# Reordering mask, copies, values and fill steps in the attention stage of a hybrid encoder kernel

## The chip, the cores and the metric

The kernel runs on one core of a Trainium2 chip. The metric is the device time of one execution in microseconds; several runs of the same kernel are taken and their median is compared. Five engines work from queues of their own: PE (matrix products; PEld is its weight load), DVE (vector), ACT (scalar functions), POOL (further vector work) and SP, which here issues the DMAs.

## What is computed

One step of an encoder layer with two branches, for a prompt of 1024 frames and for 32 new frames of a running stream that has 512 cached ones. The part that the change touches is attention, 16 heads of width 64, causal, with a bias of cumulative log forget gates:

```python
s = jnp.einsum('bqhd,bkhd->bhqk', q, k)
s = jnp.where(mask, s + bias, finfo.min)
p = jax.nn.softmax(s, axis=-1)
o = jnp.einsum('bhqk,bkhd->bqhd', p, v)
```

Beside it stand a convolution of width 31 over time (`causal_dwconv`), a layer norm over channels of its result, gates, and output projections:

```python
ya = (o_attn * silu(ga)) @ w_pa
yb = (silu(layernorm(conv, ln_g, ln_b)) * silu(gb)) @ w_pb
m = sigmoid(ma) * ya + sigmoid(mb) * yb
return x + m @ w_out
```

All arithmetic is fp32 in effect: a projection is three products of f16 or fp32r halves (`xh`·`wh`, `xh`·`wl`, `xl`·`wh`).

## The kernel before

**Stages.** First come the projections for the convolution, values, keys, queries and the attention gate (up to about 570 us), then the attention stage, then the output projections (`pa`, `pb`, `out`, from about 1052 us). In the attention stage, code written in program order sets the order on PE, DVE, ACT and SP.

**The attention stage** goes over `seq`, 132 items: for each head eight blocks of 128 queries (`Block(head, i)`, i from 0 to 7, with (i+1)·128 keys), and four items for the running stream (`Sample(g)`, four heads at a time), each put behind block 0 of heads 3, 7, 11 and 15. An item goes through these steps:

- `scores` (L1108 on): PE computes the scores into a PSUM tile `psS` (two buffers); then, in the same method, DVE adds the causal mask to the diagonal (L1124) and takes the negated row maximum `nm` (L1126).
- `soft`: ACT takes the exponential from `psS` into `P` and sums the rows (L1133).
- `norm`: DVE takes the reciprocal of the sum (L1138), POOL multiplies `P` by it (L1139).
- `turn`: PE transposes `P` in pieces of 128 keys into `psT` tiles `ptr` (L1153; two banks, up to four pieces in each). ACT copies the first bank out (L1156), DVE the second, which exists from block 4 on (the same line).
- `values`: at block 7 of a head, PE multiplies the turned blocks of the whole head with `V` (`po`, L1172) into two `psT` banks; ACT copies one half of the rows out (L1176), DVE adds the other (L1177) and, for odd heads, multiplies by the gate (L1179), which a DMA loads when block 5 comes by.
- `finish`: for the running stream alone.

The loop is a pipeline: iteration `n` does the scores, mask and maximum of item n+3, the turn of item n, the exponential of n+3, the reciprocal of n+2, two fill steps, the values of n-2, and two fill steps more.

**Fill.** `fill(n)` takes n steps from a generator that computes the remaining gate projections (`gb`, `ma`, `mb`): one step is three products of 128x352 on PE (L183). A step also calls `beat()`, which issues work that was set for that time: loads, squares and splits of weights (`junk`, `wh` on ACT, `wl` on DVE), and the taps of the convolution on DVE (L371), at a rate of `R_A` taps per step. `NFILL` gates give 528 steps in all. Twelve are taken ahead of the loop; the loop takes four per iteration, and none at blocks 0 to 2 of head 8.

**Layer norm.** Once the last tap's sums are there, each iteration also advances `layernorm()` by one step (22 steps): products with a matrix of ones into `psT` (`psn`, L1202) for mean and variance, and then Newton's steps on DVE.

```python
some = 2 if isinstance(b, Sample) or b.i > 2 or b.head.h != 8 else 0
fill(some)
if n >= 2 and pending(seq[n - 2]):
    seq[n - 2].values()
fill(some)
```

Of the kernel before, what the change touches and what calls it, by code (L numbers as in the profile page):

```python
# [8 lines left out]
F32 = mybir.dt.float32  # L9
# [5 lines left out]
ALU = mybir.AluOpType  # L15
AX = mybir.AxisListType

D = 1024
T = 1024
# [6 lines left out]
CH = 352  # L26
# [4 lines left out]
LNO = ((0,), (1, 2), (3,), (4, 5), (6,), (7,), ())  # L31
LNEXP = "natural_log_exp_and_others"
NFILL = 22
R_U, R_V, R_QK, R_G, R_A = 0.21, 0.18, 0.165, 0.23, 0.2
NWARM = 34
HT = TT // 2
HC = HT // 2
# [16 lines left out]
def build(tc, xT, xt, wv, wf, ckT, cv, clT, stT, vec, cst, yT, kT, vO, lfO, cpT, csT):  # L54
    nc = tc.nc
# [3 lines left out]
    def pool(name, bufs=1, stack=es, **kw):  # L59
        return stack.enter_context(tc.tile_pool(name=name, bufs=bufs, reuse_waits="tile", **kw))  # L60
# [19 lines left out]
    rstd = lnp.tile([128, TT], F32, name="rstd")  # L80
# [105 lines left out]
    def csl(c):  # L186
        return slice(c * CH, (c + 1) * CH)
# [88 lines left out]
    def t352(name, bufs):  # L276
        return sg.tile([128, CH], F32, name=name, tag=name, bufs=bufs)
# [5 lines left out]
    class Banks:  # L283

        n = 0
# [221 lines left out]
    def newton(out, v, y):  # L507

        nc.vector.tensor_mul(out, y, y)
        nc.vector.scalar_tensor_tensor(out, out, -0.5, v, op0=ALU.mult, op1=ALU.mult)  # L510
        nc.vector.scalar_tensor_tensor(out, out, 1.5, y, op0=ALU.add, op1=ALU.mult)
# [225 lines left out]
    for c in range(4):  # L737
# [16 lines left out]
        for t in range(8):  # L754
            ps = pj.tile([128, 512], F32, name="pjv", tag="pj")
            n = 0
            for kt in range(KT):
                sl = slice(t * 128, t * 128 + 128)
# [243 lines left out]
    psT = pool("psT", 2, stack=p2, space=PS)  # L1002
# [4 lines left out]
    class Two:  # L1007
        n = 0
# [14 lines left out]
    def fill(n):  # L1023
        for _ in range(n):
            next(flow, None)

    class Sample:
# [15 lines left out]
        def scores(self):  # L1043
            g, kc, pf = self.g, self.kc, self.pf
            ps = psS.tile([128, 2, 512], F32, name="psS", tag="S")
            for j in range(4):
                rows = slice(64 * (j % 2), 64 * (j % 2) + 64)
                q = qs_t[rows, 2 * g + j // 2, :]
                nc.tensor.matmul(ps[32 * j:32 * j + 32, 0, :], q, kc[rows, j // 2, :], start=True, stop=True)
                nc.tensor.matmul(ps[32 * j:32 * j + 32, 1, :TS], q, ks_t[rows, 2 * g + j // 2, :],  # L1050
                                 start=True, stop=True)
            nc.vector.scalar_tensor_tensor(pf[:, :PAST], ps[:, 0, :], cq[:, g:g + 1], pf[:, :PAST],
                                           op0=ALU.add, op1=ALU.subtract)
            nc.vector.scalar_tensor_tensor(pf[:, PAST:], ps[:, 1, :TS], cq[:, g:g + 1], pf[:, PAST:],
                                           op0=ALU.add, op1=ALU.subtract)
            nc.vector.tensor_add(pf[:, PAST:], pf[:, PAST:], smask)
            self.nm = nm = ap.tile([128, 3], F32, name="nm", tag="nm", bufs=6)
            nc.vector.tensor_reduce(nm[:, 0:1], pf, axis=AX.X, op=ALU.max, negate=True)
# [45 lines left out]
    class Block:  # L1104
# [5 lines left out]
        def scores(self):  # L1110
            i = self.i
            QA, QB, KA, KB = self.head.q
            nk = (i + 1) * 128
            qsl = slice(i * 128, i * 128 + 128)
            ps = psS.tile([128, 2, 512], F32, name="psS", tag="S")
            nb = 1 if nk <= 512 else 2
            w = nk // nb
            wm = max(w, 256)
            for b in range(nb):
                ksl = slice(b * w, b * w + wm)  # L1120
                nc.tensor.matmul(ps[:, b, :wm], QB[:, qsl], KB[:, ksl], start=True, stop=False)  # L1121
                nc.tensor.matmul(ps[:, b, :wm], QA[:, qsl], KA[:, ksl], start=False, stop=True)  # L1122
            diag = ps[:, nb - 1, w - 128:w]
            nc.vector.tensor_add(diag, diag, cmask)  # L1124
            nm = ap.tile([128, 3], F32, name="nm", tag="nm", bufs=6)
            nc.vector.tensor_reduce(nm[:, 0:1], ps[:, :nb, :w], axis=AX.XY, op=ALU.max, negate=True)  # L1126
            self.at = ps, nm, nk, nb, w
# [55 lines left out]
    seq = []  # L1183
# [5 lines left out]
    def start(b):  # L1189
        if getattr(b, "i", 1) == 0:  # L1190
            h = b.head
            if h.h % 2 == 0:
                h.ot = heads[h.h + 1].ot = ap.tile([128, T], F32, name="ot", tag="ot", bufs=2)
        b.scores()

    def pending(b):
        return isinstance(b, Sample) or b.i % 2

    def over_channels(acc, put):
        for c in range(3):  # L1200
            pm = psT.tile([128, 512], F32, name="psn", tag="T")
            nc.tensor.matmul(pm[:, :CH], ones_f, acc[:, csl(c)], start=True, stop=True)  # L1202
            put(csl(c), pm[:, :CH])
            yield

    def layernorm():

        shift = sides["shift"]
        for _ in range(4):
            yield  # L1210
        yield from over_channels(mean, lambda sl, ps: nc.scalar.mul(mean[:, sl], ps, 1.0 / D))

        def put(sl, ps):
            t = t352("t", 3)
            nc.scalar.activation(t, mean[:, sl], AF.Square)
            nc.vector.scalar_tensor_tensor(rstd[:, sl], ps, 1.0 / D, t, op0=ALU.mult, op1=ALU.subtract)
            nc.vector.tensor_add(mean[:, sl], mean[:, sl], shift[:, sl])
            nc.vector.tensor_scalar(rstd[:, sl], rstd[:, sl], EPS, None, op0=ALU.add)

        yield from over_channels(rstd, put)  # L1220
        for c in range(6):
            sl = slice(c * CH // 2, c * CH // 2 + CH // 2)
            v, y = rstd[:, sl], t352("t", 3)[:, :CH // 2]
            nc.scalar.activation(y, v, AF.Ln)
            nc.scalar.activation(y, y, AF.Exp, scale=-0.5)
            yield
            w = t352("t", 3)[:, :CH // 2]
            nc.vector.tensor_copy(w, v)
            newton(v, w, y)
            yield  # L1230

    ones_f = cp.tile([128, 128], F32, name="ones_f", tag="ob")
    nc.vector.memset(ones_f, 1.0)
    ln = layernorm()
    sides["shift"] = ap.tile([128, TT], F32, name="shift", bufs=1)
    nc.sync.dma_start(sides["shift"], s_m)
    heads[1].load()
    for n in range(3):
        start(seq[n])
        seq[n].soft()  # L1240
        if n:
            seq[n - 1].norm()
        fill((8, 4, 0)[n])
    for n, b in enumerate(seq):
        if n + 3 < len(seq):
            start(seq[n + 3])
        if n + 9 < len(seq) and getattr(seq[n + 9], "i", 1) == 0:
            seq[n + 9].head.load()
        if n + 6 < len(seq) and isinstance(seq[n + 6], Sample):
            seq[n + 6].load()  # L1250
        if getattr(b, "i", 0) == 3 and b.head.h + 1 < H:
            heads[b.head.h + 1].load_v()
        b.turn()
        if n + 3 < len(seq):
            seq[n + 3].soft()
        if n + 2 < len(seq):
            seq[n + 2].norm()
        some = 2 if isinstance(b, Sample) or b.i > 2 or b.head.h != 8 else 0
        fill(some)
        if n >= 2 and pending(seq[n - 2]):  # L1260
            seq[n - 2].values()
        fill(some)
        if n >= 3 and isinstance(seq[n - 3], Sample):
            seq[n - 3].finish()
        if "ready" in sides:
            next(ln, None)
# [17 lines left out]
    class Banks3:  # L1284
        n = 0
# [383 lines left out]
```

## Time and profile before

| what | value |
|---|---|
| median of 3 runs | 1349.14 us (1349.07 to 1354.99) |
| profiled execution, its own time | 1345.89 us |
| its span | 1344.1 us |
| PE busy | 1312.6 us (98%) |
| DVE busy | 990.4 us (74%) |
| ACT busy | 719.0 us (53%) |
| POOL busy | 505.8 us (38%) |
| mean granted PE clock | 0.996 |

The span is the stretch that the profiler recorded; the time of the same execution is 1.8 us longer. A group row gives line, engine, operation, output<-inputs, shapes and count, then busy time and mean duration in ns, then the engine's idle time ahead of these instructions and what ended it. A row of the timeline gives start, duration, and in brackets the idle time before it with its releaser. Matmul ends are modelled and overlap the next matmul, so that a short stall of PE may not show as idle time.

### The profile page before, as it was taken

Reading aid. Unit: us, or ns where it says so; the run is one execution under the profiler, and the core shown is the slowest. Engines: PE = TensorE matmul, PEld = TensorE weight load, DVE = VectorE, ACT = ScalarE, POOL = GpSimd, SP = SyncE. Lnnn points to the kernel's source line nnn. Section 1 sums busy time; section 2 is a strip of 40 time slices with the busy share of each in tenths; the row PEclk is TensorE's granted clock in tenths of the full one; section 3 lists DMA queues with packets and bytes.
Section 4 is the critical chain, followed back from the end, with each engine's and each line's share of the span. In section 5 each row is a group of like instructions: output and inputs, shape, how many; then the busy total and the mean of one; then the engine's idle time right before and its main releaser. Section 6 shows DMA issues by size and latency. Waiting matters only on the chain.

```text
span 1344.1 us, 24837 instructions
## 1 busy us (share of the span) xinstructions
PE 1312.6 (98%) x9383; PEld 1003.1 (75%) x9383; DVE 990.4 (74%) x1532; ACT 719.0 (53%) x1362; POOL 505.8 (38%) x548
## 2 busy tenths in 40 slices
PE   8999999999999999999889998999999999999999
PEld 5687876666666666667567766777776699999998
DVE  6797879888999997987778866655554489166664
ACT  6644555757676743455555555655555566233320
POOL 2001124547484820243433442222222158255562
PEclk8999999999999999999999999999999999999999
DMA  6343233425352463535644643565452698544462
GB/s 251 98 140 104 93 112 118 139 82 187 95 180 87 162 166 109 160 90 155 165 109 123 186 132 99 147 179 132 131 152 54 240 313 262 176 128 146 142 190 69
DMA packets 113496, 194.97 MB, mean 145 GB/s; under 512 B 34080, under 2 KB 80032, under 8 KB 113376
## 3 DMA queue, kind: packets, MB, share of 16 engines
q1 hardware_dynamic: 113232, 193.31, 46.9%
q8 instruction: 74, 1.21, 0.4%
q14 instruction: 46, 0.38, 0.1%
q10 hardware_dynamic: 144, 0.07, 0.0%
HBM read 127.68 MB, written 65.64 MB: 144 GB/s over the span
## 4 chain that ended last, share of the span: by engine, by line
PE 82%; DVE 9%; ACT 3%; issue 2%; DMA 2%; SPq 1%; POOL 0%; DVEq 0%; ACTq 0%; POOLq 0%
PE pj L183 56%; PE pjv L761 6%; PE pj L1501 6%; PE po L1172 4%; PE ptr L1153 3%; DVE nm L1126 2%; DVE wl L141 2%; DVE y L371 2%; PE psS L1122 2%; PE psS L1121 2%; DMA ga<-s_ga 2%; ACT wh L138 1%; DVE psS L1124 1%; DMA s_q<-qh 1%; PE warm L477 1%
## 5 line engine op out<-in xcount | busy, mean ns | idle before, releaser
L183 PE MATMUL pj<-xh,wh 128*128 128x352 f16 (+2 forms) x1536 | 481.6, 314 | 2.3 <-ACT wh L138 1.4
L183 PE MATMUL pj<-xh,wl 128*128 128x352 f16 (+2 forms) x1536 | 481.2, 313 | 0.7 <-DVE wl L141 0.6
L183 PE MATMUL pj<-xl,wh 128*128 128x352 f16 (+2 forms) x1536 | 480.9, 313 | 0.5 <-DVE xl L579 0.4
L183 PEld LDWEIGHTS <-wh 128*128 128x128 f16 x3072 | 301.5, 98 | 162.1 <-issue 7.1
L371 DVE SCALAR_TENSOR_TENSOR y<-u,vec_t,y 128x1086 f32<-128x1086 f32 x240 | 346.8, 1446 | 12.0 <-ACT y L368 8.9
L1139 POOL TENSOR_SCALAR P<-P,nm 128x128 f32<-128x128 f32 (+7 forms) x128 | 129.9, 1015 | 279.9 <-DVE nm L1138 229.8
L183 PEld LDWEIGHTS <-wl 128*128 128x128 f16 x1536 | 150.5, 98 | 72.0 <-DVE wl L141 1.6
L141 DVE SCALAR_TENSOR_TENSOR wl<-raw,sc,wh 128x384 f16<-128x384 f32 (+1 forms) x192 | 128.2, 693 | 48.3 <-ACT wh L138 48.3
L1133 ACT ACTIVATE P<-psS,nm 128x128 f32<-128x128 f32 (+7 forms) x128 | 95.1, 743 | 113.3 <-DVE nm L1138 70.9
L1126 DVE TENSOR_REDUCE nm<-psS 128x1 f32<-128x128 f32 (+7 forms) x128 | 97.0, 758 | 12.5
L1153 PE MATMUL ptr<-ident,P 128*128 128x128 f32 x576 | 88.6, 276 | 17.3 <-DVE pt L1156 9.2
L175 POOL TENSOR_TENSOR wl<-raw,wh 128x384 fp32r<-128x384 f32 (+1 forms) x51 | 63.3, 1270 | 74.3 <-ACT wh L172 58.6
L1153 PEld LDWEIGHTS ptr<-ident,P 128*128 128x128 f32 x576 | 69.2, 141 | 28.2 <-DVE pt L1156 12.1
L1156 ACT COPY pt<-ptr 128x512 f32<-128x512 f32 (+3 forms) x128 | 64.3, 502 | 44.4 <-PE ptr L1153 43.2
L1121 PE MATMUL psS<-KB,QB 128*128 128x256 f32 (+2 forms) x192 | 81.8, 427 | 0.6 <-ACT P L1133 0.6
L880 POOL TENSOR_TENSOR sql<-sqf,sqh 128x352 fp32r<-128x352 f32 x48 | 57.0, 1187 | 65.8 <-ACT sqh L877 65.8
L138 ACT ACTIVATE wh<-raw,sc 128x1024 f16<-128x1024 f32 (+1 forms) x68 | 73.9, 1091 | 8.2 <-DVE sc L158 7.9
L1172 PE MATMUL po<-pt,V 128*64 128x256 f32 x640 | 72.8, 382 | 2.5 <-ACT pts L1078 1.7
L1124 DVE TENSOR_TENSOR psS<-psS,cmask 128x128 f32<-128x128 f32 x128 | 37.6, 294 | 46.0 <-PE psS L1122 45.6
L906 POOL TENSOR_TENSOR ql<-qn,qh 128x352 fp32r<-128x352 f32 (+1 forms) x48 | 67.8, 1429 | 6.6 <-ACT qh L905 6.5
L761 PE MATMUL pjv<-vwh,xh 128*128 128x260 f16 x256 | 70.1, 274 | 0.0
L761 PE MATMUL pjv<-vwl,xh 128*128 128x260 f16 x256 | 70.0, 273 | 0.0
(271 smaller groups left out, 2532.9 us busy)
## 6 DMA issues: line engine op xcount, KB each, us to landing
raw<-wf SPq DMA_DIRECT2D x92, 512.0 KB
QB<-s_q SPq DMA_DIRECT2D x32, 256.0 KB
KB<-s_k SPq DMA_DIRECT2D x32, 256.0 KB
kT<-qn SPq DMA_DIRECT2D x8, 528.0 KB
s_ga<-t SPq DMA_DIRECT2D x24, 176.0 KB
s_gb<-t SPq DMA_DIRECT2D x24, 176.0 KB
s_ma<-t SPq DMA_DIRECT2D x24, 176.0 KB
s_mb<-t SPq DMA_DIRECT2D x24, 176.0 KB
```

Of the source, the lines that this page charges most:

```text
L138: nc.scalar.mul(wh[:, ks, :], raw[:, ks, :], self.s[:, i:i + 1])
L141: nc.vector.scalar_tensor_tensor(wl[:, ks, :], raw[:, ks, :], self.s[:, i:i + 1], wh[:, ks, :], op0=ALU.mult, op1=ALU.subtract)
L183: nc.tensor.matmul(ps, a[:, kt, :], b(kt, sl), start=(first and n == 0), stop=(last and n == N - 1))
L371: t = nc.vector.scalar_tensor_tensor(y, u[:, i:i + CW], w, y, op0=ALU.mult, op1=ALU.add)
L761: nc.tensor.matmul(ps[:, :VC], a, b, start=(n == 0), stop=(n == 23))
L1121: nc.tensor.matmul(ps[:, b, :wm], QB[:, qsl], KB[:, ksl], start=True, stop=False)
L1126: nc.vector.tensor_reduce(nm[:, 0:1], ps[:, :nb, :w], axis=AX.XY, op=ALU.max, negate=True)
L1133: nc.scalar.activation(P[:, :nk].rearrange("p (b w) -> p b w", b=nb), ps[:, :nb, :w], AF.Exp, bias=nm[:, 0:1], accum_out=nm[:, 1:2])
L1139: nc.gpsimd.tensor_scalar(P[:, :nk], P[:, :nk], nm[:, 2:3], 1.0, op0=ALU.mult, op1=ALU.mult)
L1153: nc.tensor.transpose(pt[:, 128 * j:128 * j + 128], P[:, 128 * (4 * u + j):128 * (4 * u + j) + 128], ident)
L1172: nc.tensor.matmul(po[rows], V[:, j, :], parts[c][:, j, :], start=(c % 2 == 0 and j < 2), stop=(c % 2 == 1 and j >= 2 * c))
L1501: nc.tensor.matmul(pss[c][:, :HC], a[:, k, :], x, start=(not more and kt == 0 and n == 0), stop=(kt == 3 and n == 2), skip_group_check=more)
```

## The change

Five things are edited in the attention stage.

- `scores` is cut in two in both classes: PE's products stay in `scores`, the mask and the maximum on DVE go to a new method `top`. In the loop `scores` of item n+3 still stands ahead of the turn of item n, `top` behind it.
- The reciprocal of item n+2 (`norm`) moves to the front of the iteration.
- `values` of item n-2 moves ahead of the exponential of item n+3 and of all fill steps.
- The four fill steps stand together; blocks 0 to 2 of head 8 get them too, and block 6 of heads 2 to 13 takes three.
- `R_A` goes from 0.2 to 0.165, and the layer norm's variance step yields between the square on ACT and the product on PE.

The loads that stood ahead of the turn now stand behind it.

```diff
-R_U, R_V, R_QK, R_G, R_A = 0.21, 0.18, 0.165, 0.23, 0.2
+R_U, R_V, R_QK, R_G, R_A = 0.21, 0.18, 0.165, 0.23, 0.165
...
                 nc.tensor.matmul(ps[:, b, :wm], QA[:, qsl], KA[:, ksl], start=False, stop=True)
+            self.at = ps, nk, nb, w
+
+        def top(self):
+            ps, nk, nb, w = self.at
             diag = ps[:, nb - 1, w - 128:w]
             nc.vector.tensor_add(diag, diag, cmask)
             nm = ap.tile([128, 3], F32, name="nm", tag="nm", bufs=6)
...
-        def put(sl, ps):
+        for c in range(3):
+            sl = csl(c)
             t = t352("t", 3)
             nc.scalar.activation(t, mean[:, sl], AF.Square)
-            nc.vector.scalar_tensor_tensor(rstd[:, sl], ps, 1.0 / D, t, op0=ALU.mult, op1=ALU.subtract)
+            yield
+            pm = psT.tile([128, 512], F32, name="psn", tag="T")
+            nc.tensor.matmul(pm[:, :CH], ones_f, rstd[:, sl], start=True, stop=True)
+            nc.vector.scalar_tensor_tensor(rstd[:, sl], pm[:, :CH], 1.0 / D, t, op0=ALU.mult, op1=ALU.subtract)
...
     for n, b in enumerate(seq):
+        if n + 2 < len(seq):
+            seq[n + 2].norm()
         if n + 3 < len(seq):
             start(seq[n + 3])
+        b.turn()
+        if n + 3 < len(seq):
+            seq[n + 3].top()
...
-        b.turn()
+        if n >= 2 and pending(seq[n - 2]):
+            seq[n - 2].values()
         if n + 3 < len(seq):
             seq[n + 3].soft()
-        if n + 2 < len(seq):
-            seq[n + 2].norm()
-        some = 2 if isinstance(b, Sample) or b.i > 2 or b.head.h != 8 else 0
-        fill(some)
-        if n >= 2 and pending(seq[n - 2]):
-            seq[n - 2].values()
-        fill(some)
+        fill(3 if getattr(b, "i", 0) == 6 and 2 <= b.head.h < 14 else 4)
```

How this moves instructions is shown at three places. On DVE, at blocks 4 and 5 of head 0 (`ptr_7044` and `ptr_7084` are the second banks of their turns), the order before was:

```order
L1124 TENSOR_TENSOR psS<-psS,cmask 128x128
L1126 TENSOR_REDUCE nm<-psS 128x1
L1156 COPY pt<-ptr_7044 128x128
L1138 RECIPROCAL nm<-nm 128x1
L141 SCALAR_TENSOR_TENSOR wl<-raw,sc,wh 128x384
L371 SCALAR_TENSOR_TENSOR y<-u,vec_t,y 128x1086
L141 SCALAR_TENSOR_TENSOR wl<-raw,sc,wh 128x384
L1124 TENSOR_TENSOR psS<-psS,cmask 128x128
L1126 TENSOR_REDUCE nm<-psS 128x1
L1156 COPY pt<-ptr_7084 128x2x128
```

and it now is, at the same two blocks (`ptr_7042`, `ptr_7082`; lines are shifted by 8):

```order
L1146 RECIPROCAL nm<-nm 128x1
L1164 COPY pt<-ptr_7042 128x128
L1132 TENSOR_TENSOR psS<-psS,cmask 128x128
L1134 TENSOR_REDUCE nm<-psS 128x1
L141 SCALAR_TENSOR_TENSOR wl<-raw,sc,wh 128x384
L371 SCALAR_TENSOR_TENSOR y<-u,vec_t,y 128x1086
L141 SCALAR_TENSOR_TENSOR wl<-raw,sc,wh 128x384
L1146 RECIPROCAL nm<-nm 128x1
L1164 COPY pt<-ptr_7082 128x2x128
```

The copy has moved ahead of mask and maximum, the reciprocal ahead of the copy; taps and weight splits stand between the maximum of one block and the reciprocal of the next, as before.

On PE, at block 1 of head 8, where the values of head 7 are computed, the order before was (no fill step follows):

```order
L1153 MATMUL ptr_9761<-ident,P 128x128 x2
L1172 MATMUL po<-pt,V 64x256 x20
L1202 MATMUL psn<-rstd,ones_f 128x352
L1121 MATMUL psS<-KB,QB 128x384
L1122 MATMUL psS<-KA,QA 128x384
```

and it now is:

```order
L1161 MATMUL ptr_9735<-ident,P 128x128 x2
L1180 MATMUL po<-pt,V 64x256 x20
L183 LDWEIGHTS wh
L183 MATMUL pj<-xh,wh 128x352
L183 LDWEIGHTS wl
L183 MATMUL pj<-xh,wl 128x352
```

Fill steps now follow the values, and the layer norm's products come between one and two heads later. At other heads two fill steps stood between the transposes and `po`; now none does.

On ACT, at the running stream's first item (its turn's copies are the two `pts` rows), the order before was:

```order
L1078 COPY pts<-ptr_7940 128x512
L1081 COPY pts<-ptr_7946 32x128
L1133 ACTIVATE P,nm<-psS,nm 128x512
L1176 COPY ot<-po 64x512 x2
L1156 COPY pt<-ptr_8001 128x2x128
```

and it now is:

```order
L1082 COPY pts<-ptr_7929 128x512
L1085 COPY pts<-ptr_7935 32x128
L1184 COPY ot<-po 64x512 x2
L1141 ACTIVATE P,nm<-psS,nm 128x512
L948 ACTIVATE t<-pj,sc 128x352
```

The exponential stands behind the two copies of `po`, so it waits for PE to finish the values.

More of the change, by code (lines that the diff above doesn't have):

```diff
@@ L1051, in scores @@
                                  start=True, stop=True)
+            self.ps = ps
+        def top(self):
+            g, ps, pf = self.g, self.ps, self.pf
             nc.vector.scalar_tensor_tensor(pf[:, :PAST], ps[:, 0, :], cq[:, g:g + 1], pf[:, :PAST],
@@ L1122, in scores, with top @@
                 nc.tensor.matmul(ps[:, b, :wm], QA[:, qsl], KA[:, ksl], start=False, stop=True)
+            self.at = ps, nk, nb, w
+        def top(self):
+            ps, nk, nb, w = self.at
             diag = ps[:, nb - 1, w - 128:w]
@@ L1211, in layernorm @@
         yield from over_channels(mean, lambda sl, ps: nc.scalar.mul(mean[:, sl], ps, 1.0 / D))
-        def put(sl, ps):
+        for c in range(3):
+            sl = csl(c)
             t = t352("t", 3)
             nc.scalar.activation(t, mean[:, sl], AF.Square)
-            nc.vector.scalar_tensor_tensor(rstd[:, sl], ps, 1.0 / D, t, op0=ALU.mult, op1=ALU.subtract)
+            yield
+            pm = psT.tile([128, 512], F32, name="psn", tag="T")
+            nc.tensor.matmul(pm[:, :CH], ones_f, rstd[:, sl], start=True, stop=True)
+            nc.vector.scalar_tensor_tensor(rstd[:, sl], pm[:, :CH], 1.0 / D, t, op0=ALU.mult, op1=ALU.subtract)
             nc.vector.tensor_add(mean[:, sl], mean[:, sl], shift[:, sl])
             nc.vector.tensor_scalar(rstd[:, sl], rstd[:, sl], EPS, None, op0=ALU.add)
-        yield from over_channels(rstd, put)
         for c in range(6):
@@ L1239, in build @@
         start(seq[n])
+        seq[n].top()
         seq[n].soft()
```

## The prediction

> **What bounds the kernel now.** I read the page's head first, then the table of windows by head, then the waits of the stage that the change touches.
>
> ```profile
> span 1344.1 us, 24837 instructions
> PE 82%; DVE 9%; ACT 3%; issue 2%; DMA 2%; SPq 1%; POOL 0%; DVEq 0%; ACTq 0%; POOLq 0%
> ```
>
> The second line is the chain of waits by engine: PE sets 82% of the end, DVE 9%. All edits lie in the attention stage, 576 to 1052 us. From the windows (PE, PEld, DVE, ACT, POOL busy with counts, then the granted clock):
>
> ```profile
> 576.00:664.00 88.00, 80.63 (x571) 58.00 (x571) 69.48 (x132) 50.12 (x108) 36.68 (x41) 1.00 0.50 137
> 664.00:785.00 121.00, 115.03 (x861) 83.08 (x861) 96.19 (x182) 64.99 (x141) 46.32 (x54) 1.00 0.49 135
> 785.00:900.00 115.00, 109.35 (x801) 79.28 (x802) 69.66 (x174) 68.65 (x154) 31.66 (x55) 0.99 0.53 143
> 900.00:1052.00 152.00, 149.86 (x1157) 108.62 (x1157) 79.70 (x194) 83.90 (x181) 36.48 (x66) 1.00 0.43 117
> 726.50:754.00 27.50, 27.41 (x198) 20.09 (x198) 23.35 (x42) 16.83 (x38) 13.27 (x14) 1.00 0.41 105
> 816.20:849.00 32.80, 28.78 (x186) 20.56 (x188) 21.68 (x53) 17.92 (x42) 7.25 (x12) 0.95 0.49 120
> ```
>
> PE idles 476 - 454.9 = 21.1 us here: 7.4 + 6.0 + 5.7 in the first three windows, 2.1 in the last. DVE is 79% busy up to 785 us (165.7 of 209), when its conv taps run, and 52% after 900. A head without disturbance (fifth row) takes 27.5 us; the head whose values end the sixth row's stretch takes 32.8, although three blocks in it have no fill. What PE waited for in the stage:
>
> ```profile
> PE ptr L1153 <- DVE pt L1156: 9.2, 11, 1.7
> PE ptr L1153 <- ACT pt L1156: 6.4, 5, 2.2
> PE po L1172 <- ACT pts L1078: 1.7, 2, 0.9
> PE ptr L1153 <- DVE ot L1177: 1.2, 1, 1.2
> PE po L1172 <- ACT mean L1211: 0.7, 1, 0.7
> PE psS L1121 <- ACT P L1133: 0.6, 2, 0.4
> ```
>
> So most of the loss is transposes (`ptr`) waiting for a `psT` bank that DVE or ACT has not yet copied out, hardly ever scores waiting for an exponential (0.6 us).
>
> **Term 1, the copy ahead of mask and maximum.** One such wait, engine by engine:
>
> ```profile
> 647.05 1.04 DVE L141 SCALAR_TENSOR_TENSOR wl<-raw,sc,wh 128x256 f16<-128x256 f32 x1
> 648.02 0.29 DVE L1124 TENSOR_TENSOR psS<-psS,cmask 128x128 f32<-128x128 f32 x1
> 648.41 1.22 DVE L1126 TENSOR_REDUCE nm<-psS 128x1 f32<-128x1024 f32 x1
> 649.55 0.28 DVE L1156 COPY pt<-ptr 128x128 f32<-128x128 f32 x1
> 649.89 0.33 PE L1153 MATMUL ptr<-ident,P 128*128 128x128 f32 x1 [1.16 <-DVE pt L1156]
> ```
>
> The copy of block 4 stands 1.53 us (648.02 to 649.55) behind a mask and maximum for another block. Moved ahead, it would have ended before PE asked. The other starts:
>
> ```profile
> 590.97 0.29 DVE L1124 TENSOR_TENSOR psS<-psS,cmask 128x128 f32<-128x128 f32 x1
> 591.57 0.41 DVE L1156 COPY pt<-ptr 128x256 f32<-128x256 f32 x1
> 592.04 0.55 PE L1153 MATMUL ptr<-ident,P 128*128 128x128 f32 x3 [1.74 <-DVE pt L1156]
> 691.24 0.29 DVE L1124 TENSOR_TENSOR psS<-psS,cmask 128x128 f32<-128x128 f32 x1
> 691.97 0.55 DVE L1156 COPY pt<-ptr 128x384 f32<-128x384 f32 x1
> 692.57 0.66 PE L1153 MATMUL ptr<-ident,P 128*128 128x128 f32 x4 [1.27 <-DVE pt L1156]
> ```
>
> Block 5's copy gains only 0.60 us and block 6's 0.73, since the maximum in front belongs to a small block. By these three amounts, four waits for block 4's copy vanish, three for block 5's lose 0.5 us each, four for block 6's 0.68 each: about 7 of the 9.2 us (told apart by the number of transposes that waited: 1 or 2, 3, 4). From below the term is 0 (PE comes earlier to a DVE that is just as busy). I take 5.5, near the upper end, because the waits after a block are single and short, and a copy in front is in front every time.
>
> **Term 2, the fill steps.** Four steps are twelve matmuls:
>
> ```profile
> 742.25 1.79 PE pj L183 x12
> 816.20 4.11 PE L1172 MATMUL po<-pt,V 128*64 128x256 f32 x36 [0.65 <-ACT mean L1211]
> 823.48 0.52 PE L1153 MATMUL ptr<-ident,P 128*128 128x128 f32 x3 [1.25 <-DVE ot L1177]
> 824.57 0.86 PE L1202 MATMUL psn<-rstd,ones_f 128*128 128x352 f32 x2 [0.57 <-ACT pt L1156]
> 834.27 0.33 PE L1153 MATMUL ptr<-ident,P 128*128 128x128 f32 x1 [2.20 <-ACT pt L1156]
> 826.00:828.00 2.00, 2.00 (x9) 1.45 (x9) 0.64 (x2) 1.33 (x4) 0.80 (x1) 0.50 0.89 199
> ```
>
> A step is 1.79 / 4 = 0.45 us. Head 8's three empty blocks get 12 steps, 5.4 us of PE work, where PE idled 0.65 + 1.25 + 0.57 + 2.20 = 4.7 us and where the granted clock fell (last row: 0.50 for 2 us, so 1 us more). Twelve other heads give up one step each at block 6. If head 8's stalls took up the work whole, the gain would be 5.4 us plus that 1 us; if the givers are held by DVE anyway, as the heads before 785 us partly are, only half of the twelve pay. I take 4.5, bounds 2 and 6.5. [...]
>
> **Term 3, values ahead of the whole fill.** PE now goes from the turn's transposes straight to `po`, with two fill steps (0.9 us) less for the copies, and four steps instead of two behind it. The wait of 1.25 at 823.48 (already counted) shows what four steps behind would cover. Against it stands the one place without fill ahead, the 0.65 us at 816.20. Worst are the four running-stream blocks, whose turn uses both `psT` banks:
>
> ```profile
> 663.27 0.58 ACT L1078 COPY pts<-ptr 128x512 f32<-128x512 f32 x1
> 663.90 4.54 PE L1172 MATMUL po<-pt,V 128*64 128x256 f32 x40 [0.94 <-ACT pts L1078]
> ```
>
> ACT is late there by itself, so the wait grows by the whole 0.9 us at the two blocks that wait today and by 0 to 0.9 at the other two: -1.8 to -3.6, taken as -2.7. The twelve plain heads need their second bank only after the first six of twenty products (0.3 of 4.54 us, 1.4 us later), so I put 0.1 us on each, bounds 0 and 0.65: -1.2 (0 to -7.8).
>
> **Term 4, reciprocal first, pace, layer norm.** R_A from 0.2 to 0.165 takes 0.035 x 4 = 0.14 taps from each block while taps last:
>
> ```profile
> L371 DVE SCALAR_TENSOR_TENSOR y<-u,vec_t,y x41: 1328/1333/2207, 579.5 to 772.7; 128x1086 f32<-128x1086 f32 x41
> 649.75 1.12 ACT L1133 ACTIVATE P<-psS,nm 128x1024 f32<-128x1024 f32 x1 [1.79 <-DVE nm L1126]
> 641.19 0.52 PE L1121 MATMUL psS<-KB,QB 128*128 128x512 f32 x1
> 642.24 0.60 PE L1153 MATMUL ptr<-ident,P 128*128 128x128 f32 x4
> L138 ACT ACTIVATE wh<-raw,sc 128x1024 f16<-128x1024 f32 x22 | 25.1, 1140 | 0.0
> L1133 ACT ACTIVATION_READ_ACCUMULATOR P<-psS,nm 128x1 f32 x128 | 25.0, 195 | 0.0
> L1138 DVE RECIPROCAL nm<-nm 128x1 f32<-128x1 f32 x128 | 19.6, 153 | 0.2 <-ACT P L1133 0.2
> ```
>
> At 1.33 us a tap that is 0.19 us per block, some 11 us of DVE time over the 57 blocks until 772 us, given back after it, where DVE has room; the last taps and the 22 layer-norm steps still end well inside the 132 blocks. What PE gets of it is between 0 and the 4 us of DVE waits that the first two windows would otherwise keep or see return; I take +2. The reciprocal, 0.15 us, never waited before (0.2 us over 128). At the head of DVE's block it can: it waits for the exponential of two blocks on, and copy, mask and maximum wait behind it. At block 4 the loop is copy 0.28, mask and maximum 1.53, exponential 1.12, accumulator 0.2, reciprocal 0.15: 3.3 us. PE's own block is the fill's 1.79, four score products (641.19 to 642.24, 1.05) and five transposes, about 0.6: 3.4. They nearly tie, so I charge 0.03 us for each of 64 blocks with a DVE copy, -2; from 0 to -20 (0.31 each). The layer norm's extra yield moves a wait of DVE for a square; PE does not see it. No DMA is added; the loads of a head come one turn later on SP, with several blocks to spare, and the fill steps after 1052 us are the same.
>
> **Sum.** 5.5 + 4.5 - 2.7 - 1.2 + 2 - 2 = 6.1 us from single waits. The displayed idle of 21.1 leaves out what a stall hides under the modelled tails of matmuls: the 32.8 us after 816.2 lack six fill steps (the other six lie before it), so they are 32.8 - (27.5 - 2.7) = 8.0 over a plain head, of which 1.3 are three `psn` products (0.86 for two passes, some half of it tail) and 1 the clock: 5.7, against 4.0 displayed in it (1.25 + 0.57 + 2.20). That ratio is 1.4; I let the 10 us of terms 1 and 2 grow by 1.3, to 13, and the sum to 9. On the profiled execution 1344.1 becomes 1335 (its time 1345.9 becomes 1337). The median of the runs, 1349.1, lies 3.2 above that one, so I forecast 1349 - 9 = **1340 us**.
>
> **Rivals.** (a) *The banks were the whole trouble*: DVE's copy waits, ACT's (6.4 us) and the hole all go, about 21 of idle less 4 of new waits: 1349 - 18 = 1331. For it: the clean head at 27.5 us with DVE 85% busy. Against: the ACT waits have other causes. (b) *The copy does not come sooner where it counts*: in rows like 591.57 taps and `wl` stand ahead of mask and copy alike, term 1 gives 2 and the new `po` waits 5; with the hole 4.5 and the pace 2 that leaves 3.5: 1345.5. For it: the longest wait, 1.74, keeps 1.1 even by my own count. (c) *The loop decides, and it is slower*: reciprocal, copy, maximum and exponential form a ring through DVE and ACT, and at the end of a head the exponential also stands behind two copies of `po` on ACT, 4.5 us later. If each of 64 large blocks loses 0.14 us beyond the 0.03 charged (the 9 us), the gain is gone; at 0.31 the kernel stands at 1349 - 9 + 20 = 1360. For it: the tie above, and 22 `wh` splits of 1.14 us on the same ACT queue. Against: scores have two buffers and waited 0.6 us in all, and blocks 0 to 3 need no DVE copy, so a lag is made good there. [...]
>
> **How the numbers follow.** My forecast (1335 to 1345) has 0.50, (a) 0.15, (b) 0.22, (c) 0.13. What a measurement of this kernel tells from no change is about 0.5%, 6.7 us: faster means below 1342.4, slower above 1355.9. Faster takes 0.47 of the 0.50 and all of (a): 0.62; same is the rest and (b): 0.25; slower is (c): 0.13. For 8 in 10 the range goes from inside (a), 1329, to beyond (b), 1351.
>
> **What would show it.** Right: PE's waits for DVE `pt` fall from 9.2 below 4 us, the granted clock stays 1.00 around head 8, its stretch of 32.8 us shrinks below 30, and `po` <- ACT `pts` rises by 2 to 3 us. Wrong: reciprocals or copies on DVE with idle time put down to ACT's exponential, scores waiting for ACT `P` by many times 0.6 us, or new `po` waits at plain heads beyond 0.3 us each; and if the stage's idle falls while its length does not, the sum from displayed waits was the mistake.

## The result and the profile after

The changed kernel takes 1361.32 us (median of 5 runs, 1360.73 to 1363.06), the one before 1350.59 (5 runs, 1349.07 to 1354.99): a ratio of 1.0074, 95% interval 1.0052 to 1.0097. It is slower by some 10 us; 1340 was forecast, and the time lies where rival (c) stood. The profiled execution, at 1363.1 us, is the longest of the five, while that of the kernel before, at 1345.9, is shorter than all of its five, so the two traces lie 17 us apart where the medians lie 11 apart. Sizes are therefore taken from ratios below, and the traces are used to see where things moved.

From the page of the changed kernel, its span and the chain of waits by engine:

```profile
span 1361.3 us, 24814 instructions
PE 78%; DVE 8%; ACT 4%; DMA 4%; issue 3%; SPq 2%; POOL 0%; DVEq 0%; ACTq 0%; POOLq 0%
```

PE's share of the chain fell from 82 to 78%. The loss is in the attention stage, which here runs from 576 to 1069 us; the columns are the stretch, its length, busy time of PE, PEld, DVE, ACT and POOL with counts, the granted clock, DMA share and GB/s:

```profile
576.00:1069.00 493.00, 463.51 (x3392) 331.29 (x3392) 315.56 (x684) 266.58 (x582) 122.64 (x215) 0.99 0.47 127
```

It is 17 us longer than the 476 before. PE's idle time rose from 21.1 to 29.5 us, and PE's busy time by another 8.7 for the same matmuls (3392 records and 3386). What PE waited for there:

```profile
PE po L1180 <- ACT pts L1082: 8.0, 4, 2.7
PE ptr L1161 <- ACT pt L1164: 7.2, 9, 1.6
PE psS L1125 <- ACT P L1141: 3.5, 5, 1.1
PE po L1180 <- ACT pt L1164: 2.5, 4, 1.3
PE ptr L1161 <- ACT mean L1219: 2.2, 2, 1.2
PE ptr L1161 <- DVE pt L1164: 1.7, 2, 1.2
PE ptr L1084 <- ACT pt L1164: 1.6, 1, 1.6
```

The wait for DVE's copy fell from 9.2 to 1.7 us, just as term 1 had it. Head 8's stretch, from the values of head 7 at 821.0 to its own at 851.2 us, takes 30.2 us where it took 32.8, and its clock stays at 1.00. In their place stand waits for ACT: for the running stream's copy (`pts`) 8.0 instead of 1.7, at plain heads 2.5 for the second bank (`po` <- ACT `pt`) instead of none, for the turned copies 7.2 instead of 6.4, and scores waiting for an exponential 3.5 instead of 0.6. Some 5 of the 8.7 us of busy time are the clock, by an estimate from the slices below (6.5 us lost, less 1.7 before). These are slices of the changed kernel at three of the four running-stream items:

```profile
660.00:670.00 10.00, 5.83 (x27) 3.25 (x29) 6.35 (x9) 4.31 (x10) 5.18 (x8) 0.69 0.86 196
910.00:920.00 10.00, 7.93 (x50) 5.11 (x50) 4.50 (x14) 4.67 (x12) 1.81 (x5) 0.83 0.70 168
1030.00:1040.00 10.00, 7.49 (x46) 4.74 (x48) 3.67 (x10) 4.07 (x11) 1.46 (x4) 0.83 0.12 41
```

The granted clock is 0.69, 0.83 and 0.83 there, over ten us each: 3.1 + 1.7 + 1.7 = 6.5 us of clock lost. Before, one slice of the stage alone had such a clock, at head 8, for 1.7 us:

```profile
820.00:830.00 10.00, 8.18 (x40) 5.42 (x37) 6.34 (x14) 3.40 (x7) 1.01 (x2) 0.83 0.34 100
```

The first of the three places, in the timeline (start, duration, engine, instruction, idle time before it and its releaser):

```profile
659.25 0.60 PE L1081 MATMUL ptr<-ident,pf 128*128 128x128 f32 x4
...
659.84 1.35 DVE L371 SCALAR_TENSOR_TENSOR y<-u,vec_t,y 128x1086 f32<-128x1086 f32 x1 [1.88 <-ACT y L368]
...
661.45 0.29 PE L1084 MATMUL ptr<-ident,pf 128*32 128x128 f32 x1 [1.61 <-ACT pt L1164]
...
662.22 0.58 ACT L1141 ACTIVATE P<-psS,nm 128x384 f32<-128x384 f32 x1 [0.81 <-DVE nm L1134]
662.69 0.19 ACT L1141 ACTIVATION_READ_ACCUMULATOR P<-psS,nm 128x1 f32 x1
662.79 1.04 ACT L117 ACTIVATE junk<-raw 128x1024 bf16<-128x1024 f32 x1
...
663.83 0.57 ACT L1082 COPY pts<-ptr 128x512 f32<-128x512 f32 x1
...
664.45 7.52 PE L1180 MATMUL po<-pt,V 128*64 128x256 f32 x40 [2.71 <-ACT pts L1082]
```

ACT copies the turn's first bank 4 us after PE filled it: it stands behind an exponential that itself waited for DVE's maximum, and behind a square of weights (`junk`). DVE was late with that maximum because a tap of the convolution stood in front, which had itself waited 1.88 us for ACT. PE has only `po` next, so it idles 1.61 and 2.71 us with one transpose between, and then the values run at the reduced clock (0.69 from 660 to 670 us): 7.52 us where the same 40 records took 4.54 before.

### The profile page after: what moved, and what is told of

It reads as the page before. It is cut to its first block, busy times and chain, and to the rows that moved or that the text cites. A ratio compares the mean times of both kernels' runs of the same rounds, so it can differ in the third digit from the quotient of the medians.

```text
span 1361.3 us, 24814 instructions
## 1 busy us (share of the span) xinstructions
PE 1320.1 (97%) x9383; PEld 1004.8 (74%) x9383; DVE 987.4 (73%) x1532; ACT 716.3 (53%) x1362; POOL 475.0 (35%) x548
## 4 chain that ended last, share of the span: by engine, by line
PE 78%; DVE 8%; ACT 4%; DMA 4%; issue 3%; SPq 2%; POOL 0%; DVEq 0%; ACTq 0%; POOLq 0%
PE pj L183 54%; PE pjv L761 6%; PE pj L1512 6%; PE po L1180 4%; PE ptr L1161 3%; DMA ga<-s_ga 2%; DVE nm L1134 2%; PE psS L1125 2%; PE psS L1126 2%; ACT wh L138 1%; DVE wl L141 1%; DVE y L371 1%; DMA s_y<-y 1%; ACT P L1141 1%; DVE psS L1132 1%
## 5 line engine op out<-in xcount | busy, mean ns | idle before, releaser
L1147 POOL TENSOR_SCALAR P<-P,nm 128x128 f32<-128x128 f32 (+7 forms) x128 | 95.8, 749 | 277.7 <-DVE nm L1146 220.2
L1180 PE MATMUL po<-pt,V 128*64 128x256 f32 x640 | 80.3, 407 | 10.6 <-ACT pts L1082 8.0
L1180 PEld LDWEIGHTS po<-pt,V 128*64 128x64 f32 x640 | 46.8, 145 | 40.0 <-ACT pts L1082 9.1
L761 PE MATMUL pjv<-vwh,xl 128*128 128x260 f16 x256 | 69.9, 273 | 0.0
```

What stands on the lines that cost most here:

```text
L761: nc.tensor.matmul(ps[:, :VC], a, b, start=(n == 0), stop=(n == 23))
L1147: nc.gpsimd.tensor_scalar(P[:, :nk], P[:, :nk], nm[:, 2:3], 1.0, op0=ALU.mult, op1=ALU.mult)
L1180: nc.tensor.matmul(po[rows], V[:, j, :], parts[c][:, j, :], start=(c % 2 == 0 and j < 2), stop=(c % 2 == 1 and j >= 2 * c))
```

## The experiments

All ratios are to the kernel before, run on the same chip in turn with it. The expectations name theories: S (the four running-stream items lose cover and clock), V (values first cost at every head, through the exponential behind two copies of `po`), L (the loop of reciprocal, copy, maximum and exponential, rival (c)).

**e1: values back between the fill steps, in the changed kernel.**

```diff
-        if n >= 2 and pending(seq[n - 2]):
-            seq[n - 2].values()
         if n + 3 < len(seq):
             seq[n + 3].soft()
-        fill(3 if getattr(b, "i", 0) == 6 and 2 <= b.head.h < 14 else 4)
+        some = 3 if getattr(b, "i", 0) == 6 and 2 <= b.head.h < 14 else 4
+        fill(2)
+        if n >= 2 and pending(seq[n - 2]):
+            seq[n - 2].values()
+        fill(some - 2)
```

> The changed kernel with one part undone: values stand between two fill steps and the rest again, and the exponential ahead of them on ACT; all else as changed. Theory S (the four running-stream items: po waits 8.0 us for ACT's pts copy where it waited 1.7, and the granted clock falls to 0.50 for some 5 us behind three of them): both go back, 1361 to about 1349, po's wait for pts under 2.5 us and no slice of the clock below 0.9 in the attention stage. Theory L (the loop of reciprocal, copy, maximum, exponential on all large blocks): the time stays within 3 us of 1361, since the loop is left as it is.

Measured: 1351.25 us, ratio 1.0004 (0.9993 to 1.0016). PE's wait for `pts` fell to 4.0 us, and in the profiled execution, the shortest of ten, only one slice of ten us in the stage (830 to 840) has a clock below 0.98. The place of the values is worth some 9 us; `pts` stayed above the 2.5 that was expected. What is left of the change gains nothing on the kernel before.

**e2: two fill steps ahead of the values at the running stream's items alone, in the changed kernel.**

```diff
+        some = 3 if getattr(b, "i", 0) == 6 and 2 <= b.head.h < 14 else 4
+        if isinstance(b, Sample):
+            fill(2)
+            some -= 2
         if n >= 2 and pending(seq[n - 2]):
             seq[n - 2].values()
         if n + 3 < len(seq):
             seq[n + 3].soft()
-        fill(3 if getattr(b, "i", 0) == 6 and 2 <= b.head.h < 14 else 4)
+        fill(some)
```

> The changed kernel, with two of the four fill steps put ahead of the values only in the four iterations whose turn is a running-stream item. Theory S: nearly as good as undoing it everywhere, 1349 to 1352, since 0.9 us more at these places lets ACT finish its pts copy and keeps the clock up. Theory V (values right behind the turn cost at every head, by the exponential behind two po copies on ACT): at most a third of the loss returns, 1357 or more. Theory L: within 3 us of 1361.

Measured: 1353.93 us, ratio 1.0025 (1.0012 to 1.0037), 2 us above what S expected and 3 below V. Four iterations out of 132 carry some 0.5 of the 0.7% that e1 wins; what is left for the plain heads is 0.2%, with intervals that just overlap. In e2's trace, these are the values at the third item and the slice around it:

```profile
910.97 4.54 PE L1180 MATMUL po<-pt,V 128*64 128x256 f32 x40 [1.18 <-ACT pts L1082]
```

```profile
905.00:915.00 10.00, 8.82 (x71) 6.07 (x70) 5.46 (x16) 5.11 (x13) 2.01 (x6) 1.00 0.70 172
```

The wait is 0.9 us shorter than in the changed kernel (2.07), the price of the two steps, and the clock stays at 1.00. The fourth item's clock is back at 1.00 as well, but not the first's: there the wait is 1.82 instead of 2.71 us, the clock still falls to 0.66 in the slice from 660, and the values take 7.21 us. In e1 the same wait left the clock at 1.00 (last section), so that fall is not what tells e2 from e1 by its edit.

**e3: values first alone, in the kernel before.**

```diff
         b.turn()
+        if n >= 2 and pending(seq[n - 2]):
+            seq[n - 2].values()
         if n + 3 < len(seq):
             seq[n + 3].soft()
...
-        fill(some)
-        if n >= 2 and pending(seq[n - 2]):
-            seq[n - 2].values()
-        fill(some)
+        fill(2 * some)
```

> The kernel before with the values alone moved ahead of the exponential and of all fill steps. Theories S and V: slower than before by 8 to 15 us, with po waiting 6 us or more for pts and the clock at 0.50 behind stream items. Theory L: within 4 us of before, since reciprocal and maximum stay where they were.

Measured: 1359.31 us, ratio 1.0073 (1.0047 to 1.0100): the edit alone costs what the whole change does. PE's wait for `pts` is 5.0 us in four places (6 or more was expected), and plain heads wait 1.3 us more. The clock did not fall behind the running stream's items, as S and V had it: the only slice below 0.98 stands ahead of the first one (0.83, 650 to 660 us), and the four executions have a mean granted clock of 0.9940 where those of the kernel before beside them have 0.9933. The stage, up to the last values, in e3's trace:

```profile
576.00:1062.90 486.90, 458.04 (x3395) 329.50 (x3395) 318.80 (x682) 269.52 (x582) 154.54 (x215) 1.00 0.47 129
```

PE idles 28.9 us in it, against 21.1 before, so here the loss is waiting in the main, and not the clock.

**e10: the exponential ahead of the values again, in the changed kernel.**

```diff
+        if n + 3 < len(seq):
+            seq[n + 3].soft()
         if n >= 2 and pending(seq[n - 2]):
             seq[n - 2].values()
-        if n + 3 < len(seq):
-            seq[n + 3].soft()
```

> The changed kernel with the exponential ahead of the values again; the values still stand straight behind the turn's transposes, with no fill ahead. Theory C (cover: PE reaches po before ACT has copied the turn out): the loss stays, 1357 to 1362, and po's wait for pts stays above 6 us. Theory E (the exponential behind two po copies on ACT): at least half of the 10 us that e1 wins comes back, 1356 or less.

Measured: 1361.63 us, ratio 1.0091 (1.0074 to 1.0108). Nothing comes back, and `pts` stays at 7.5 us: theory V's mechanism (E in the expectation), the exponential behind two copies of `po`, is out. What is missing is the cover between the turn and `po` (C in the expectation).

**e4: mask and maximum behind the turn alone, in the kernel before.**

```diff
         if n + 3 < len(seq):
             start(seq[n + 3])
...
         b.turn()
+        if n + 3 < len(seq):
+            seq[n + 3].top()
```

(with `scores` cut in two as in the change). 

> The kernel before with the mask and maximum alone moved behind the turn, so that DVE's copy comes first. By the prediction's term 1: PE's wait for DVE pt falls from 9.2 us to about 2, and the time is 5 to 7 us below before. Theory L: that wait falls too, but the exponential comes later on ACT, PE's waits for ACT pt and ACT P rise by as much or more, and the time is the same or up to 10 us above before.

Measured: 1353.63 us, ratio 1.0016 (1.0003 to 1.0030). PE's waits in its attention stage:

```profile
PE ptr L1161 <- ACT pt L1164: 9.7, 9, 3.5
PE ptr L1161 <- DVE pt L1164: 4.0, 5, 1.3
```

DVE `pt` falls by 5.2 us and ACT `pt` rises by 3.3, with further small waits for ACT: theory L's picture. The gain of term 1 does not reach the end.

**e5, e6, e7: fill spread, reciprocal first, lower pace, each alone in the kernel before.**

```diff
-        some = 2 if isinstance(b, Sample) or b.i > 2 or b.head.h != 8 else 0
-        fill(some)
+        some = 3 if getattr(b, "i", 0) == 6 and 2 <= b.head.h < 14 else 4
+        fill(2)
         if n >= 2 and pending(seq[n - 2]):
             seq[n - 2].values()
-        fill(some)
+        fill(some - 2)
```

> The kernel before with the fill steps alone spread (four at blocks 0 to 2 of head 8, three at block 6 of heads 2 to 13, values still between them). Term 2 of the prediction: 4 to 6 us below before, the granted clock 1.00 around head 8. Rival: the work put into the hole was covered by nothing else, but the stalls there belong to the layer norm's products in the same blocks; then the stalls stay or move and the time is within 2 us of before.

```diff
     for n, b in enumerate(seq):
+        if n + 2 < len(seq):
+            seq[n + 2].norm()
...
-        if n + 2 < len(seq):
-            seq[n + 2].norm()
```

> The kernel before with the reciprocal alone moved to the front of the iteration. Theory L (DVE's queue stands behind a reciprocal that waits for ACT's exponential): 2 to 10 us above before, with idle time of DVE before the reciprocal of several us in place of 0.2. Rival: it costs nothing, within 2 us of before, since DVE waits for PE's scores at that point anyway.

```diff
-R_U, R_V, R_QK, R_G, R_A = 0.21, 0.18, 0.165, 0.23, 0.2
+R_U, R_V, R_QK, R_G, R_A = 0.21, 0.18, 0.165, 0.23, 0.165
```

> The kernel before with the pace of the taps alone lowered, 0.2 to 0.165. Term 4: 0 to 4 us below before, PE's waits for DVE pt fewer than 9.2 us. Rival: later taps push the layer norm's products off the three blocks without fill into blocks with fill, and the gain or loss comes from there: the waits around head 8 shrink, by 2 us or more, while those before 785 us stay.

Measured: e5 1349.36 us, ratio 0.9990 (0.9975 to 1.0004); e6 1350.37, 1.0004 (0.9994 to 1.0014); e7 1345.73, 0.9962 (0.9949 to 0.9976). So the spread fill alone is worth nothing that can be told, the reciprocal alone nothing, the pace alone 5 us. In e6's trace DVE does stand 35.8 us before reciprocals that wait for the exponential, as theory L said, and no cost shows. In e5's trace, one of its longer executions (1352.58 us), the slice with a low clock at head 8 is gone, but three others appear, of which the first is

```profile
650.00:660.00 10.00, 8.84 (x54) 4.92 (x52) 6.19 (x15) 4.68 (x10) 5.59 (x5) 0.66 0.51 128
```

In e7 the layer norm's `psn` products move off the blocks without fill (809 to 830 us before):

```profile
L1202 PE MATMUL psn<-mean,ones_f x6: 459/459/459, 861.1 to 868.0; 128*128 128x352 f32 x6
L1202 PE MATMUL psn<-rstd,ones_f x6: 459/459/459, 875.5 to 882.8; 128*128 128x352 f32 x6
```

That is the half of its rival that came. The other half did not: PE's idle time from 785 to 900 us went from 5.7 to 6.9 us, while that up to 785 us, where the taps run, fell from 13.3 to 10.0, nearer to term 4's own account. DVE `pt` waits stay in sum (8.8 us, 9.2 before). But e7's profiled execution was its longest, with nearly the span of the one before (1344.3 and 1344.1 us), so the trace does not show where the 5 us come from.

**e8: values and mask back, in the changed kernel** (left are spread fill, pace, reciprocal first, the layer norm's yield).

```diff
         if n + 3 < len(seq):
             start(seq[n + 3])
+        if n + 3 < len(seq):
+            seq[n + 3].top()
         b.turn()
-        if n + 3 < len(seq):
-            seq[n + 3].top()
```

(and the edit of e1). 

> The changed kernel with values between the fill steps and mask and maximum ahead of the turn again; left are the spread fill, the pace, the reciprocal in front and the layer norm's yield. If the copy ahead of mask and maximum costs something through ACT (alone it stood at a ratio of 1.0016 to before), this is 1 to 4 us below e1's 1351.3 and below before; if term 1 gains, it is 3 us or more above e1, with DVE pt waits back at some 7 us.

Measured: 1342.25 us, ratio 0.9935 (0.9915 to 0.9955): 8 us better than before and 9 below e1. The copy ahead of mask and maximum, which alone cost about 2 us, costs 9 in the changed kernel's company, more than the 1 to 4 us expected. DVE `pt` waits are back at 9.7 us, and it does not matter.

**e9: lower pace, spread fill and yield, in the kernel before** (the edits of e5 and e7 with the layer norm's).

> The kernel before with the lower pace, the spread fill and the layer norm's yield; reciprocal, mask, maximum and values where they were. Against e8 (ratio 0.9935 to before) only the reciprocal differs. If the gain of e8 is the pace and the fill together, this is 1342 to 1345, ratio 0.993 to 0.996. If the reciprocal in front is needed for it (POOL's scaling beside mask and maximum and not beside taps), this is no better than the pace alone, ratio 0.9962 or above.

Measured: 1342.87 us, ratio 0.9946 (0.9931 to 0.9961), which cannot be told from e8 (where the loads also stand one turn later): the reciprocal in front is not needed for the gain. The yield was not run by itself.

**e11: e1 with the reciprocal back behind the exponential.**

```diff
-        if n + 2 < len(seq):
-            seq[n + 2].norm()
         if n + 3 < len(seq):
             start(seq[n + 3])
...
             seq[n + 3].soft()
+        if n + 2 < len(seq):
+            seq[n + 2].norm()
```

> Kernel e1 (values between the fill steps) with the reciprocal also back behind the exponential; the copy still stands ahead of mask and maximum. Theory R (a ring on DVE: reciprocal waits for the exponential, the copy behind it, mask and maximum behind the copy): the cost of the copy in front falls with the reciprocal gone, and this is 5 us or more below e1's 1351.3, near e8. Theory A (mask and maximum behind the copy delay the exponential on ACT, and with it ACT's next copy, wherever the reciprocal stands): within 3 us of e1, and PE's wait for ACT pt stays near 7 us.

Measured: 1344.39 us, ratio 0.9959 (0.9944 to 0.9974), 6 us below e1 by the ratios. This is what theory R expected: neither the reciprocal in front nor the copy in front costs more than some 2 us, both together cost 8 (e9 to e1). The groups of DVE and ACT in the stage, of e1 and then of e11:

```profile
L1146 DVE RECIPROCAL nm<-nm 128x1 f32<-128x1 f32 x125 | 19.8, 158 | 39.8 <-ACT P L1141 39.3
L1164 DVE COPY pt<-ptr 128x128 f32<-128x128 f32 (+1 forms) x64 | 30.6, 479 | 13.6 <-PE ptr L1161 13.5
L1141 ACT ACTIVATE P<-psS,nm 128x640 f32<-128x640 f32 (+3 forms) x124 | 92.7, 748 | 147.9 <-DVE nm L1134 123.0 <-DVE sc L157 10.1 <-PE ptr L1161 8.8
```

```profile
L1146 DVE RECIPROCAL nm<-nm 128x1 f32<-128x1 f32 x125 | 19.1, 153 | 2.1 <-ACT P L1141 2.1
L1164 DVE COPY pt<-ptr 128x128 f32<-128x128 f32 (+1 forms) x64 | 31.2, 487 | 31.9 <-PE ptr L1161 31.3
L1141 ACT ACTIVATE P<-psS,nm 128x512 f32<-128x512 f32 (+3 forms) x125 | 93.6, 749 | 137.3 <-DVE nm L1146 132.2 <-PE ptr L1161 4.4 <-DVE nm L1069 0.6
```

In e1 DVE stands 39.8 us before reciprocals that wait for ACT's exponential, and ACT stands 147.9 us before exponentials that in the main wait for DVE: each holds the other. With the reciprocal back the first figure is 2.1 and the second 137.3. Neither figure is a loss by itself. This is the reciprocal in e8, the fastest of these kernels:

```profile
L1146 DVE RECIPROCAL nm<-nm 128x1 f32<-128x1 f32 x125 | 19.7, 158 | 30.0 <-ACT P L1141 29.6
```

What PE loses shows in its waits for ACT's copies `pt`: 10.7 us in all in e1 (7.6 and 1.6 at transposes, 1.1 at `tot`, 0.4 at `po`) against 4.1 in e11. That the two moves together cost 8 us is measured; that the ring of waits is how they do it is the reading of these rows.

**e12: e8 with mask and maximum behind the turn at block 4 alone.**

```diff
+        late_top = getattr(b, "i", 0) == 4
-        if n + 3 < len(seq):
+        if n + 3 < len(seq) and not late_top:
             seq[n + 3].top()
         b.turn()
+        if n + 3 < len(seq) and late_top:
+            seq[n + 3].top()
```

> Kernel e8 with mask and maximum behind the turn at block 4 only, where the maximum ahead of the copy is the longest (1.53 us with its mask) and the copy the shortest (0.28 us). Theory A with the prediction's own prices: the copy comes 1.5 us sooner, the exponential only some 0.3 to 1 us later, so it is the one block where the swap could pay: 0 to 4 us below e8, about 1340. If the swap costs there as well, 1 to 3 us above e8.

Measured: 1345.08 us, ratio 0.9965 (0.9952 to 0.9978), some 4 us above e8, with intervals that just touch. The swap costs, if anything, even where the prediction's prices spoke most for it.

Five of these kernels form a ladder with the changed one, each step adding about one piece. Waits and idle times are from the attention stage of each trace, the clock is the mean over a kernel's executions (0.9933 to 0.9940 for the kernel before beside them):

| kernel | added | ratio to before | mean granted clock | transposes wait for DVE `pt`, us | for ACT `pt`, us | DVE idle ahead of reciprocals, us | ACT idle ahead of exponentials, us |
|---|---|---|---|---|---|---|---|
| e7 | lower pace | 0.9962 | 0.9966 | 8.8 | 4.7 | 0.5 | 110.8 |
| e9 | spread fill, yield | 0.9946 | 0.9950 | 9.1 | 3.1 | 0.8 | 105.0 |
| e8 | reciprocal first | 0.9935 | 0.9962 | 9.7 | 3.4 | 30.0 | 112.7 |
| e11 | (e9 and copy first) | 0.9959 | 0.9965 | 1.6 | 4.1 | 2.1 | 137.3 |
| e1 | e8 and copy first | 1.0004 | 0.9956 | 2.1 | 7.6 | 39.8 | 147.9 |
| changed | values first | 1.0074 | 0.9920 | 1.7 | 7.2 | 40.3 | 129.2 |

## Why the prediction was wrong

**Term 1 was right in the wait and wrong in what it is worth.** DVE `pt` fell by 7.5 us, within 0.5 of the count by block. The step that failed is to take such waits as time won ("I take 5.5, near the upper end, because the waits after a block are single and short"): the mask and maximum that the copy overtakes release ACT's exponential, and ACT makes the other half of the turned copies. Alone (e4) the edit costs some 2 us; from e8 to e1 it removes 7.6 us of waits for DVE and makes the kernel 0.7% slower, some 9 us. Moving work on an engine that two others wait for only moved the wait.

**The loop of term 4 was seen, and priced too low.** The prediction charged 2 us, because loop (3.3 us) and PE's own block (3.4) tie. In company with the copy first, the reciprocal first costs 6 us (e11 to e1), alone nothing (e6). The bound of 20 held; the choice near its lower end did not. The sum of durations left out what the prediction named under rival (c) alone: ACT's queue also carries weight splits and squares (1.14 and 1.05 us), so that a tie on average is a loss wherever one of these falls into the loop. That last point is read from the timeline above and was not tried by itself.

**Term 3 had the waits at `po` about right, and not what they cost.** It put 2.7 us on the running stream's items and 1.2 on the plain heads. In e3, where nothing else moves, the waits for `pts` grew by 3.3 us and those at plain heads by 1.3. But transposes waited another 2.5 us for copies, PE's idle time in the stage grew by 7.7, and the kernel lost some 10 us. The factor of 1.3 for stalls that the trace does not display was put on the gains of terms 1 and 2 and not on these losses.

In the changed kernel term 3 and the other moves met at the running stream's items. ACT copies the turn's first bank 4.0, 0.3, 1.6 and 1.9 us after PE filled it at the four items; before it was 1.3, 1.2, 0.0 and 0.3, and in e3 it is the same as before, so this lateness does not come from the values. The waits came to 8.0 us, and behind three of the four the granted clock fell (to 0.69, 0.83 and 0.83 over ten us), so that 4.54 us of values took up to 7.52. Undoing the two steps there (e2) shortens the third item's wait by 0.9, from 2.07 to 1.18, as priced. In place of -3.9 the values first cost about 9 us (e1 to the changed kernel, 0.7%; 0.5% of it at four items, by e2). The prediction used the row with a clock of 0.50 only for a gain at head 8 and never asked where its own new waits might bring the same.

**Term 2 was mis-sized.** It was put at 4.5 us; alone it measured 1.3 (interval from -3.4 to +0.5 us), and with the yield on top of the pace 2 (from ratios whose intervals overlap). The filled hole kept its clock (1.00 from 820 to 850 us in e5), but in e5's profiled execution three other slices of ten us fell to 0.66, 0.83 and 0.83; over its ten executions the mean clock is 0.9949, no lower than that of the kernel before beside them (0.9940). **The pace** was put at 2 us and measured 5.

So the gains of 5.5 + 4.5 + 2 were in truth about 9 (e8: the pace, the fill with the yield, and the reciprocal in front, which costs nothing there), and the losses of 6 were about 19 (e8 to the changed kernel). Rival (c), at 0.13, named the mechanism of half of that. That its price of 1360 was met is in part luck: it had no term for the clock, its part with the exponential behind `po` came to nothing (e10), and it counts the 2 us already charged twice, without which it is 1358. (Rival (a) takes 4 from 21 and subtracts 18.) Of the signs of being right, the fall of DVE `pt` and head 8's clock came, while `pts` rose by 6.3 us in place of 2 to 3. Of the signs of being wrong, "scores waiting for ACT `P` by many times 0.6 us" and reciprocals idle for ACT's exponential (40.3 us in the changed kernel) both came, though e6 and e8 have such idle reciprocals without a loss.

How much of this is clock can be estimated from the mean granted clocks on record: 0.001 of it over 1350 us is 1.35 us. From e1 (0.9956) to the changed kernel (0.9920) that is some 5 of the values' 9 us, so by this estimate about half is clock and half wait; in e3 none of the 10 us is. For the pace alone (0.9966, and 0.9940 for the kernel before beside it) it is some 3.5 of the 5 us. What stays open is where in the stage the pace's gain arises, and why transposes wait longer in e3.

The version to keep is e8 or e9, at 0.9935 and 0.9946 of the kernel before: spread fill, lower pace and the layer norm's yield, without the other moves.

## What to carry to other kernels

When an instruction is moved ahead of another on one engine, price the one that is overtaken as well: ask which third engine its result releases, and what else that engine does for the first. A queue that waits for another which waits for it can turn two nearly harmless moves into one costly pair (here 2 us or less apart and 8 together), so try such edits together and apart. Filler between a producer and the instruction that needs its copied result is not slack: two steps of 0.45 us at four places out of 132 carried half a per cent.

## What the runs showed of the hardware

Behind some of PE's waits of 1.8 to 2.7 us at `po` the granted clock fell, so that the wait was not the whole cost. This is the changed kernel just behind the first running-stream item, where it fell to 0.50:

```profile
663.00:665.00 2.00, 0.55 (x4) 0.36 (x6) 2.00 (x3) 1.54 (x4) 2.00 (x3) 0.68 1.04 258
665.00:667.00 2.00, 2.00 (x12) 1.12 (x10) 0.78 (x2) 0.00 (x0) 1.21 (x4) 0.50 1.07 236
667.00:669.00 2.00, 2.00 (x12) 1.18 (x10) 0.68 (x1) 0.58 (x1) 0.20 (x1) 0.50 1.03 219
669.00:671.00 2.00, 2.00 (x14) 1.10 (x13) 0.00 (x0) 0.00 (x0) 0.20 (x1) 0.61 1.02 242
```

PE is nearly idle for 4.3 us ahead of the values at 664.45 (1.61 and 2.71, with one transpose between) and fully busy from there on, and the clock is 0.50, 0.50 and 0.61 in the rows from 665 to 671 us. In these runs it did not follow from the length of the wait alone: behind a wait of 2.07 us it fell to 0.83 over ten us in the changed kernel (the slice from 910 above), and behind one of the same 2.07 us in e10 it did not:

```profile
910.00:920.00 10.00, 7.93 (x65) 5.39 (x63) 4.76 (x15) 5.44 (x14) 2.00 (x6) 1.00 0.68 165
```

The clearest pair is e1 and e2 at the first item. In both, two fill steps stand ahead of the values there. From the item's scores (657.25 us) up to the values PE's rows agree to 0.01 us, with waits of 1.60 and 1.82 us in both; then the clock stays at 1.00 in e1 and falls to 0.66 over ten us in e2. The values and the slice, of e1 and then of e2:

```profile
663.02 4.54 PE L1180 MATMUL po<-pt,V 128*64 128x256 f32 x40 [1.82 <-ACT pts L1082]
660.00:670.00 10.00, 8.16 (x65) 5.37 (x66) 6.39 (x11) 5.08 (x12) 6.02 (x10) 1.00 0.97 236
```

```profile
663.02 7.21 PE L1180 MATMUL po<-pt,V 128*64 128x256 f32 x40 [1.82 <-ACT pts L1082]
660.00:670.00 10.00, 8.16 (x47) 4.58 (x47) 4.93 (x7) 3.35 (x8) 5.18 (x8) 0.66 0.99 233
```

So the same wait had both outcomes: at 1.82 us a clock of 1.00 or 0.66, at 2.07 us of 1.00 or 0.83, each over ten us. What decides between them was not shown by any run here.
